# Two token tiles of the output projection written ahead of the last head of the first attention, and each tile's mixed heads loaded during the tile before it

## The chip, the cores and the metric

The kernel runs on one core of one Trainium2 chip. A core has five engines with instruction streams of their own: TensorE (matrix products, into PSUM), VectorE, ScalarE, GpSimd and SyncE; in the profile they are PE, DVE, ACT, POOL and SP, and PEld is TensorE's loading of the stationary operand. SyncE only issues DMAs here; GpSimd issues DMAs and does some elementwise work. Each engine runs its instructions in the order in which they stand in its stream, and waits at an instruction until the semaphores it needs are there. The metric is the device time of one execution in microseconds (us).

## The reference

A decoder block over 2048 tokens of width 1024, in float32, depth 1:

```python
ada = c_act @ ada_w[l] + ada_b[l]                  # shift, scale, gate of both sub-layers
h = rms_norm(x, pre_norm_mix[l]) * (1.0 + sc_a) + sh_a
proj = h @ w_in                                     # one projection for both groups of heads
go = gla_chunked(gq, gk, gv, g_log)                 # 4 heads, gated linear attention
go = from_heads(rms_norm(go, gla_norm)) * jax.nn.silu(g_og)
do = diff_attention(dq, dk, dv, lam)                # 4 heads, (softmax1 - lam * softmax2) @ V, causal
do = from_heads(rms_norm(do, diff_norm) * (1.0 - lambda_init))
y = jnp.concatenate([go, do], axis=-1) @ w_out      # the output projection
x = x + gt_a * rms_norm(y, post_norm_mix[l])
h = rms_norm(x, pre_norm_mlp[l]) * (1.0 + sc_m) + sh_m
y = jnp.square(jax.nn.relu(h @ w_up[l])) @ w_down[l]
x = x + gt_m * rms_norm(y, post_norm_mlp[l])
```

The output projection of a token needs all eight mixed heads of that token. An attention head of a block of 128 queries reads the keys and values of all tokens up to the block's end.

## The kernel before

Float32 products are made of three products of split operands (high × high, high × low, low × high), each of 128 × 128 by up to 512 columns. The 2048 tokens are 16 **token tiles** of 128 and four **groups** of 512 (group t has tiles 4t to 4t + 3).

The stages, in the order in which they are written: the input projection with the linear attention for groups 0 and 1, then for groups 2 and 3; the differential attention of groups 0 and 1 (the *first attention*, begun among the last input projections); the output projection, most of it written among the differential attention of groups 2 and 3 (the *second attention*); the rest of the output projection; the MLP (from L1035 on). The change concerns only the attentions and the output projection.

**An attention** (`attention`, L171) is a generator. Its steps are (group t, head h, block j of 128 queries), and a step of group t has t + 1 chunks of 512 keys. Each turn of the innermost loop is a *tick*, after which the generator yields: scores of one chunk of the present step on TensorE (`qk`, `S`, L214), whose PSUM bank VectorE moves out with the running maximum (L219, or L222 for the chunk on the diagonal); then, for the step two steps back (`lag` 2), the transposes of the probabilities of one chunk (`turn`, L263), copied out by ScalarE (L265), and one tick later the products with V (`pv`, `O`, L274). After the last chunk of a step come the exponentials on ScalarE (L232) and the combination of the two softmaxes on VectorE (L238). When the last block of a head is done, `norm` (L279) makes squares on ScalarE, a root and `don` on VectorE (L289); two ticks later `finish` (L292) transposes `don` (L297), splits it (L299, L300), stores it to the scratch tensor `mixS` through GpSimd's queue (L302), and enters the head (t, h) in the set `finished`. Keys, values and queries are loaded by SyncE two steps ahead (L190, L192, L202).

**The output projection** (`out_proj`, L915) is a generator with 16 steps for a token tile: two halves `b` of 512 columns, eight rows `k` of w_out, each step with three matmuls (`Y`, L931 to L933). Ahead of a tile's steps stand the load of its mixed heads (`mx`, L921; in two parts for tiles 12 to 15, the last head by itself) and of the residual `xt` (L923), both on SyncE's queue. `mx` has two buffers; `xt` and `yt` share three with the raw rows of w_out. The two halves of a tile take two PSUM banks of one tag, of which there are two, so that the next tile's first matmul needs this tile's eviction. Behind the matmuls: squares on ScalarE (L936), a root and two evictions `wyt` on VectorE (L944), the sum with the residual on GpSimd (L946; on VectorE from tile 11 on), the store of x1, a second norm (L950, L952) and the store of `xnS`.

**What sets the order.** The program text interleaves generators by hand. `interleave` (L1003) takes one tick of the attention and then as many projection steps as are due: two a tick for the first 48 ticks of the second attention, then 1.5, at most 11 tiles (`TB`), and none while the next tile in the order `TOKS` (L964) isn't `ready`, which means that all four heads of its group are in `finished`. By the time `interleave` begins on the first attention, all but its last three ticks have been written: two a step of the last input projection (L867), two a row of w_out as this is split (L905). `prep_first` (L966), also driven a tick at a time, makes the first operands of the MLP out of finished tiles; it waits for counts of projection steps.

The order on the engines isn't quite the written one. A scheduler in the program builder places the instructions: among those that it reckons ready, it takes the one written first, so that an instruction written later can stand earlier in an engine's stream. That order is fixed before the kernel runs.

Of the kernel before, what the change touches and what calls it, by code (L numbers as in the profile page):

```python
# [9 lines left out]
F32 = mybir.dt.float32  # L10
F32R = mybir.dt.float32r
# [8 lines left out]
P = 128  # L20
# [3 lines left out]
NH = 4  # L24
# [3 lines left out]
NTOK = S // P  # L28
# [6 lines left out]
AT0 = 2  # L35
GA1 = 4
WL = 2
RA = 2.0
RB = 2.0
RC = 1.5  # L40
GA0 = 22
# [8 lines left out]
def tile_hybrid_block(  # L50
# [3 lines left out]
    nc = tc.nc  # L54
# [12 lines left out]
    mixS = [dram.tile([P, 4, 2 * NH, 2, P], F32, name=f"mixS{t}") for t in range(NT)]  # L67
# [49 lines left out]
    def rsqrt_col(pool, ss, n, inv_n, tag):  # L117

        y = pool.tile([P, n], F32, tag=tag + "y", name=tag + "y", bufs=2)
        nc.scalar.activation(y, ss, AF.Ln, scale=inv_n, bias=eps_c)  # L120
        nc.scalar.activation(y, y, AF.Exp, scale=-0.5)
        v = pool.tile([P, n], F32, tag=tag + "v", name=tag + "v", bufs=2)
        nc.vector.tensor_scalar(v, ss, inv_n, EPS, op0=ALU.mult, op1=ALU.add)

        w = pool.tile([P, n], F32, tag=tag + "w", name=tag + "w", bufs=2)
        nc.vector.tensor_tensor(w, y, y, op=ALU.mult)
        nc.vector.scalar_tensor_tensor(w, w, -0.5, v, op0=ALU.mult, op1=ALU.mult)
        r = pool.tile([P, n], F32, tag=tag + "r", name=tag + "r", bufs=2)
        nc.vector.scalar_tensor_tensor(r, w, 1.5, y, op0=ALU.add, op1=ALU.mult)
        return r  # L130
# [37 lines left out]
    finished = set()  # L168
# [273 lines left out]
    def run(g, n=None):  # L442

        while n is None or n > 0:
            if next(g, run) is run:
                return False
            n = None if n is None else n - 1
        return True
# [416 lines left out]
    at = attention((0, 1), sa, 1024, 6, pp, atags, 3, 3, 2)  # L865
# [26 lines left out]
    sw = c1.enter_context(tc.tile_pool(name="p1w", bufs=2, side="left", reuse_waits="tile"))  # L892
# [11 lines left out]
    for k in range(NK):  # L904
# [7 lines left out]
        if k + 3 < NK:  # L912
            load_wo(k + 3)

    def out_proj(tiles):  # L915

        for tk in tiles:
            assert all((tk // 4, h) in finished for h in range(NH))
            mx = sw.tile([P, 2 * NH, 2, P], F32R, tag="mx", name="mx", bufs=2)
            for ks in (slice(0, 7), slice(7, 8)) if tk >= 12 else (slice(0, 8),):  # L920
                nc.sync.dma_start(mx[:, ks].bitcast(F32), mixS[tk // 4][:, tk % 4, ks])  # L921
            xt = sw.tile([P, D], F32, tag="wx", name="wxt", bufs=3)
            nc.sync.dma_start(xt, x[tk * P:(tk + 1) * P, :])  # L923
            yps = []
            ss = sw.tile([P, 2], F32, tag="wss", name="wss", bufs=2)
            for b in range(2):
                yp = pp.tile([P, 512], F32, tag=("C" if tk > 12 and tk % 2 else "A"), name="Y",
                             bufs=4 if tk > 12 and tk % 2 else 2)
                cs = slice(512 * b, 512 * b + 512)
                for k in range(NK):  # L930
                    nc.tensor.matmul(yp, mx[:, k, 0, :], wohi[k][:, cs], start=(k == 0), stop=False)  # L931
                    nc.tensor.matmul(yp, mx[:, k, 0, :], wolo[k][:, cs], start=False, stop=False)  # L932
                    nc.tensor.matmul(yp, mx[:, k, 1, :], wohi[k][:, cs], start=False, stop=(k == NK - 1))  # L933
                    yield
                junk = sw.tile([P, 512], BF16, tag="wjunk", name="wjunk", bufs=1)
                nc.scalar.activation(junk, yp, AF.Square, accum_out=ss[:, b:b + 1])  # L936
                yps.append(yp)
            s1 = sw.tile([P, 1], F32, tag="ws1", name="ws1", bufs=2)
            nc.vector.tensor_tensor(s1, ss[:, 0:1], ss[:, 1:2], op=ALU.add)
            r = rsqrt_col(sw, s1, 1, 1.0 / D, "wr")  # L940
            yt = sw.tile([P, D], F32, tag="wx", name="wyt", bufs=3)
            for b in range(2):
                cs = slice(512 * b, 512 * b + 512)
                nc.vector.scalar_tensor_tensor(yt[:, cs], yps[b], r, gtg[:, cs], op0=ALU.mult, op1=ALU.mult)  # L944
            eng = nc.vector if tk >= 11 else nc.gpsimd
            eng.tensor_tensor(xt, xt, yt, op=ALU.add)  # L946
            nc.gpsimd.dma_start(x1S[tk], xt)

            s2 = sw.tile([P, 1], F32, tag="ws2", name="ws2", bufs=2)
            nc.scalar.activation(yt, xt, AF.Square, accum_out=s2)  # L950
            r2 = rsqrt_col(sw, s2, 1, 1.0 / D, "wq")
            nc.vector.tensor_scalar(yt, xt, r2, None, op0=ALU.mult)  # L952
            nc.gpsimd.dma_start(xnS[tk // 8][:, tk % 8], yt.rearrange("p (k c) -> p k c", c=P))
# [7 lines left out]

    TOKS = (0, 4, 1, 5, 2, 6, 3, 7) + tuple(range(8, 16))  # L964

    def prep_first(pool, tag):  # L966


        for n in range(16):
            i, k = n // 4, n % 4  # L970
            while len(wsteps) < 32 * (i + 1) + 4:
                yield
            raw = pool.tile([P, 2, 2, P], F32, tag="prq", name="xnq", bufs=2)
            for j in range(2):
                nc.gpsimd.dma_start(raw[:, j], xnS[0][:, 4 * j + i].rearrange("p (e k) c -> p e k c", e=2)[:, :, k, :])
            for _ in range(3):
                yield
            ps = pp.tile([P, 2, 2, P], F32, tag=tag, name="ntr", bufs=4)
            for e in range(2):
                for j in range(2):  # L980
                    nc.tensor.transpose(ps[:, e, j, :], raw[:, j, e, :], ident)
            bt = pool.tile([P, 2, 2, P], F32, tag="prq", name="hBq", bufs=2)
            for e in range(2):
                kk = k + 4 * e
                nc.scalar.activation(bt[:, e], ps[:, e], AF.Identity, bias=cols[:, 24 + kk:25 + kk],
                                     scale=prem[:, 1, kk:kk + 1])
# [12 lines left out]

    TB = 11  # L1000
    op = out_proj(TOKS[:TB])

    def interleave(at, first, rate, later, pre=None):  # L1003


        due, i = 0.0, 0
        while run(at, 1):
            due += rate if i < first else later
            while due >= 1.0:
                if len(wsteps) == 16 * TB or not ready(TOKS[len(wsteps) // 16]):  # L1010
                    due = 0.0
                    break
                run(op, 1)
                wsteps.append(1)
                due -= 1.0
            if pre is not None:
                run(pre, 1)
            i += 1

    wsteps = []  # L1020

    def ready(tk):
        return all((tk // 4, h) in finished for h in range(NH))

    interleave(at, 0, RA, RA)
    cA.close()
    cA = ExitStack()
    sa = cA.enter_context(tc.tile_pool(name="pA1", bufs=2, side="right", reuse_waits="tile"))
    at = attention((2, 3), sa, S, 6, pp, atags, 5, 5, 2)
    pre = prep_first(sa, "C")  # L1030
    interleave(at, 48, RB, RC, pre)
    run(op)
    run(pre)
# [109 lines left out]


    op = out_proj(TOKS[TB:])
    fetch_op(0)
    run(op, 14)
# [74 lines left out]
    n = len(usteps)  # L1222
    ready_ops = {}
    prep_todo = [(k, hf) for k in range(4) for hf in range(2)]
    for s, (g, c, wi, p) in enumerate(usteps):
        i = WORD[wi]
# [17 lines left out]
        nm, first = BANK[i]  # L1244
# [320 lines left out]
```

## Time and profile before

| what | value |
|---|---|
| time, median of 3 runs | 2588.66 us (2583.26 to 2590.06) |
| time of the profiled execution | 2586.39 us |
| its span, first to last instruction | 2584.7 us |
| mean granted TensorE clock | 0.983 |
| first and last `Y` matmul | 833.7 us, 1318.4 us |
| issues of `mx` loads | 20, from 824.2 to 1304.4 us |

The profile is of one execution. A busy engine is one that has an instruction under way; the idle time in front of an instruction is put down to the instruction or DMA that came last of those it waited for. The granted clock is the share of TensorE's full clock that it had in a stretch. Times in the trace are counted from the span's start.

### The profile page before, as it was taken

The page shows a single profiled execution, that of the slowest core. Times are in us where ns is not written, and L with a number is a line of the kernel's source. Part 1 is how long each engine was busy: PE and PEld are TensorE (multiplying, and loading weights), DVE is VectorE, ACT ScalarE, POOL GpSimd, SP SyncE. Part 2 cuts the span into 40 slices and gives each one's busy share as a digit, 9 for nine tenths or more (in the row PEclk, how much of TensorE's full clock was granted, in tenths as well). Part 3 has the DMA queues.
Part 4 walks back from the last instruction along what each step waited for, and adds up shares of the span by engine and source line. Part 5 has one row for each costly group of instructions (what it writes and reads, how often), then busy time and mean ns, then how long its engine had stood idle before and what let it go on. Part 6 is the DMA issues. An engine that isn't in the chain of part 4 may idle for free.

```text
span 2584.7 us, 35418 instructions
## 1 busy us (share of the span) xinstructions
PE 2464.8 (95%) x12532; PEld 2050.6 (79%) x12532; DVE 1593.1 (62%) x3111; ACT 1150.2 (45%) x2185; POOL 442.9 (17%) x654
## 2 busy tenths in 40 slices
PE   5899999999998899999999999999999999999998
PEld 4777787877787688888778888788888888788886
DVE  6535855247864677777577767866664445543756
ACT  4352224313444565566555555645553333222444
POOL 2211322102321123332012322112111000100000
PEclk8999999999999999999999999999999999999999
DMA  7354551444844766665475655744438767855856
GB/s 263 110 186 134 192 188 58 131 133 149 253 135 154 221 200 204 214 208 170 170 249 199 229 197 175 234 145 167 142 136 285 264 201 239 277 172 166 288 167 209
DMA packets 218792, 491.61 MB, mean 190 GB/s; under 512 B 24848, under 2 KB 78800, under 8 KB 217072
## 3 DMA queue, kind: packets, MB, share of 16 engines
q1 hardware_dynamic: 170000, 329.12, 40.3%
q0 software_dynamic: 48608, 160.16, 16.7%
q8 instruction: 100, 1.64, 0.3%
q14 instruction: 84, 0.69, 0.1%
HBM read 329.79 MB, written 159.39 MB: 189 GB/s over the span
## 4 chain that ended last, share of the span: by engine, by line
PE 41%; issue 17%; DMA 3%; POOL 3%; DVE 2%; ACT 2%; POOLq 0%; SPq 0%; DVEq 0%; ACTq 0%
PE dn L1428 4%; PE dn L1430 4%; PE dn L1429 4%; PE upY L1253 2%; PE upY L1251 2%; PE upY L1252 2%; PE S L214 2%; PE O L274 2%; PE Y L933 2%; PE Y L931 2%; PE Y L932 2%; PE upX L1253 2%; PE upV L1251 2%; PE upV L1253 2%; PE upV L1252 2%
## 5 line engine op out<-in xcount | busy, mean ns | idle before, releaser
L1428 PE MATMUL dn<-dnhi,uhi 128*128 128x512 f32 x880 | 344.5, 391 | 3.9 <-DVE du L1408 3.9
L1430 PE MATMUL dn<-dnhi,ulo 128*128 128x512 f32 x880 | 344.1, 391 | 1.1 <-DVE ulo L1357 1.1
L1429 PE MATMUL dn<-dnlo,uhi 128*128 128x512 f32 x880 | 344.2, 391 | 0.0
L1355 ACT CAST uhi<-us 128x1024 fp32r<-128x1024 f32 (+1 forms) x126 | 118.7, 944 | 359.8 <-PE dn L1429 343.2
L1357 DVE TENSOR_TENSOR ulo<-us,uhi 128x1024 fp32r<-128x1024 f32 (+1 forms) x126 | 136.9, 1087 | 160.6 <-ACT uhi L1355 155.9
L537 PE MATMUL projt<-hThi,whi 128*128 128x512 f32 x512 | 207.2, 405 | 0.6 <-DVE cols L416 0.6
L538 PE MATMUL projt<-hTlo,whi 128*128 128x512 f32 x512 | 206.3, 403 | 0.0
L539 PE MATMUL projt<-hThi,wlo 128*128 128x512 f32 x512 | 202.0, 395 | 2.2 <-DVE wlo L471 2.2
L1428 PEld LDWEIGHTS dn<-dnhi,uhi 128*128 128x128 f32 x880 | 165.9, 189 | 39.8 <-issue 3.6
L1430 PEld LDWEIGHTS dn<-dnhi,ulo 128*128 128x128 f32 x880 | 166.0, 189 | 36.6 <-DVE ulo L1357 1.5
L1429 PEld LDWEIGHTS dn<-dnlo,uhi 128*128 128x128 f32 x880 | 166.0, 189 | 35.3
L232 ACT ACTIVATE P<-P,nm 128x128 f32<-128x128 f32 (+15 forms) x128 | 153.7, 1201 | 48.9 <-DVE nm L222 48.1
L214 PE MATMUL S<-K,q 128*128 128x512 f32 (+3 forms) x640 | 169.7, 384 | 2.6 <-issue 1.6
L1133 ACT CAST wuhi<-wA 128x512 fp32r<-128x512 f32 x160 | 99.1, 619 | 163.9 <-PE upV L1252 69.2
L274 PEld LDWEIGHTS O<-V,PTs 128*128 128x128 f32 x1088 | 141.5, 193 | 26.4 <-ACT PTs L265 15.6
L274 PE MATMUL O<-V,PTs 128*128 128x128 f32 x1088 | 151.9, 280 | 8.4 <-ACT PTs L265 4.9
L1253 PE MATMUL upY<-hhi,wulo 128*128 128x512 f32 x384 | 151.6, 395 | 2.0 <-DVE wulo L1134 2.0
L1251 PE MATMUL upY<-hhi,wuhi 128*128 128x512 f32 x384 | 151.7, 395 | 0.2 <-ACT wuhi L1133 0.2
L1252 PE MATMUL upY<-hlo,wuhi 128*128 128x512 f32 x384 | 151.5, 394 | 0.0
L551 PE MATMUL projn<-whi,hThi 128*128 128x256 f32 x512 | 147.7, 288 | 3.4 <-DVE cols L416 2.6
L552 PE MATMUL projn<-wlo,hThi 128*128 128x256 f32 x512 | 146.9, 287 | 0.0
L553 PE MATMUL projn<-whi,hTlo 128*128 128x256 f32 x512 | 145.5, 284 | 0.0
(334 smaller groups left out, 5727.1 us busy)
## 6 DMA issues: line engine op xcount, KB each, us to landing
us<-uS SPq DMA_DIRECT2D x94, 512.0 KB, 4.2
wA<-in_w_up_dram SPq DMA_DIRECT2D x128, 256.0 KB, 3.1
uS<-t POOLq DMA_DIRECT2D x128, 256.0 KB, 3.2
wraw<-in_w_in_dram SPq DMA_DIRECT2D x48, 512.0 KB, 4.6
uS<-c POOLq DMA_DIRECT2D x96, 256.0 KB, 3.1
K<-kS SPq DMA_DIRECT2D x40, 512.0 KB, 5.4
wds<-in_w_down_dram SPq DMA_DIRECT2D x78, 256.0 KB, 4.2
adaraw<-in_ada_w_dram SPq DMA_DIRECT2D x32, 512.0 KB, 4.0
```

The costliest lines, as they stand in the source:

```text
L214: nc.tensor.matmul(ps[:, :wd], qt[:, m, hl, qs], Kc[ci][:, m, :wd], start=(hl == 0), stop=(hl == 1))
L232: nc.scalar.activation(Ps[m][:, :width], Ps[m][:, :width], AF.Exp, scale=-1.0, bias=nms[m][:, t:t + 1], accum_out=sums[:, 0, m:m + 1])
L274: nc.tensor.matmul(outs[t, h][:, j, :], pt[:, kb % 4, :], Vc[g][:, kb % 4, :], start=(kb == 0), stop=(kb == nb - 1))
L537: nc.tensor.matmul(ps, whi[k][:, cs], hi[:, k, :], start=(k == 0), stop=False)
L538: nc.tensor.matmul(ps, whi[k][:, cs], lo[:, k, :], start=False, stop=False)
L539: nc.tensor.matmul(ps, wlo[k][:, cs], hi[:, k, :], start=False, stop=(k == NK - 1))
L1251: nc.tensor.matmul(ps, whi[:, k, :], hi[:, k, :], start=(first and k == 0), stop=False, skip_group_check=not first)
L1252: nc.tensor.matmul(ps, whi[:, k, :], lo[:, k, :], start=False, stop=False, skip_group_check=not first)
L1253: nc.tensor.matmul(ps, wlo[:, k, :], hi[:, k, :], start=False, stop=(k == 3), skip_group_check=not first)
L1428: nc.tensor.matmul(banks[t], uhi[:, tk], whi, start=first, stop=False, skip_group_check=on)
L1429: nc.tensor.matmul(banks[t], uhi[:, tk], wlo, start=False, stop=False, skip_group_check=on)
L1430: nc.tensor.matmul(banks[t], ulo[:, tk], whi, start=False, stop=last, skip_group_check=on)
```

## The change

The load of `mx` becomes a function of its own, `load_mx`. In a tile's step (b, k) = (1, 0), the ninth of 16, the text now asks for the next tile's `mx`, if the heads of its group are finished. The order of the tiles begins 0, 1, 4, 5 in place of 0, 4, 1, 5, and the counts in `prep_first` are those that fit it. In the last three ticks of the first attention, `interleave` is replaced by a loop that writes 16 projection steps after each tick until 32 are written: tile 0 after the first, tile 1 after the second, both ahead of the third, in which `finish` of head (1,3) falls. In the second attention, a tile whose `mx` hasn't been asked for is asked for in a tick, and its first step is written three ticks later at the earliest.

```diff
-RA = 2.0
...
+    def load_mx(tk):
+
+        if tk in mxs or not ready(tk):
+            return
+        mxs[tk] = sw.tile([P, 2 * NH, 2, P], F32R, tag="mx", name="mx", bufs=2)
+        for ks in (slice(0, 7), slice(7, 8)) if tk >= 12 else (slice(0, 8),):
+            nc.sync.dma_start(mxs[tk][:, ks].bitcast(F32), mixS[tk // 4][:, tk % 4, ks])
+
     def out_proj(tiles):
 
-        for tk in tiles:
-            assert all((tk // 4, h) in finished for h in range(NH))
-            mx = sw.tile([P, 2 * NH, 2, P], F32R, tag="mx", name="mx", bufs=2)
-            for ks in (slice(0, 7), slice(7, 8)) if tk >= 12 else (slice(0, 8),):
-                nc.sync.dma_start(mx[:, ks].bitcast(F32), mixS[tk // 4][:, tk % 4, ks])
+        for n_, tk in enumerate(tiles):
+            load_mx(tk)
+            mx = mxs.pop(tk)
...
+                    if (b, k) == (1, 0):
+                        at_ = TOKS.index(tk) + 1
+                        if at_ < NTOK:
+                            load_mx(TOKS[at_])
                     yield
...
-    TOKS = (0, 4, 1, 5, 2, 6, 3, 7) + tuple(range(8, 16))
+    TOKS = (0, 1, 4, 5, 2, 6, 3, 7) + tuple(range(8, 16))
...
-            while len(wsteps) < 32 * (i + 1) + 4:
+            while len(wsteps) < (48, 64, 96, 128)[i] + 4:
...
+    def op_step():
+
+        if len(wsteps) == 16 * TB or (len(wsteps) % 16 == 0 and TOKS[len(wsteps) // 16] not in mxs):
+            return False
+        run(op, 1)
+        wsteps.append(1)
+        return True
+
+    def interleave(at, first, rate, later, pre):
+
+
+        due, i, asked = 0.0, 0, {}
         while run(at, 1):
             due += rate if i < first else later
+            n = len(wsteps) // 16
+            if len(wsteps) % 16 == 0 and n < TB and TOKS[n] not in mxs:
+                load_mx(TOKS[n])
+                asked[n] = i
             while due >= 1.0:
-                if len(wsteps) == 16 * TB or not ready(TOKS[len(wsteps) // 16]):
+                n = len(wsteps) // 16
+                if (len(wsteps) % 16 == 0 and i < asked.get(n, -3) + 3) or not op_step():
                     due = 0.0
                     break
...
-    interleave(at, 0, RA, RA)
+    load_mx(0)
+    while run(at, 1):
+        for _ in range(16):
+            if len(wsteps) < 32:
+                op_step()
```

More of the change, by code (lines that the diff above doesn't have):

```diff
@@ L913, in tile_hybrid_block, with ready @@
             load_wo(k + 3)
-    def out_proj(tiles):
-        for tk in tiles:
-            assert all((tk // 4, h) in finished for h in range(NH))
-            mx = sw.tile([P, 2 * NH, 2, P], F32R, tag="mx", name="mx", bufs=2)
-            for ks in (slice(0, 7), slice(7, 8)) if tk >= 12 else (slice(0, 8),):
-                nc.sync.dma_start(mx[:, ks].bitcast(F32), mixS[tk // 4][:, tk % 4, ks])
+    mxs = {}
+    def ready(tk):
+        return all((tk // 4, h) in finished for h in range(NH))
+    def load_mx(tk):
[4 more added lines that the diff above has]
+            nc.sync.dma_start(mxs[tk][:, ks].bitcast(F32), mixS[tk // 4][:, tk % 4, ks])
+    def out_proj(tiles):
+        for n_, tk in enumerate(tiles):
+            load_mx(tk)
+            mx = mxs.pop(tk)
             xt = sw.tile([P, D], F32, tag="wx", name="wxt", bufs=3)
@@ L1001, in tile_hybrid_block @@
     op = out_proj(TOKS[:TB])
-    def interleave(at, first, rate, later, pre=None):
-        due, i = 0.0, 0
+    wsteps = []
+    def op_step():
[6 more added lines that the diff above has]
+        due, i, asked = 0.0, 0, {}
         while run(at, 1):
             due += rate if i < first else later
+            n = len(wsteps) // 16
+            if len(wsteps) % 16 == 0 and n < TB and TOKS[n] not in mxs:
+                load_mx(TOKS[n])
+                asked[n] = i
             while due >= 1.0:
-                if len(wsteps) == 16 * TB or not ready(TOKS[len(wsteps) // 16]):
+                n = len(wsteps) // 16
+                if (len(wsteps) % 16 == 0 and i < asked.get(n, -3) + 3) or not op_step():
                     due = 0.0
                     break
-                run(op, 1)
-                wsteps.append(1)
                 due -= 1.0
-            if pre is not None:
-                run(pre, 1)
+            run(pre, 1)
             i += 1
-    wsteps = []
-    def ready(tk):
-        return all((tk // 4, h) in finished for h in range(NH))
-    interleave(at, 0, RA, RA)
+    load_mx(0)
[3 more added lines that the diff above has]
+                op_step()
     cA.close()
```

## The prediction, on record before the result

> **What bounds the kernel now.** I read the page first, then the waits of TensorE around the end of the first attention, then the instructions in order of time there, and last the busy time by stretches.
>
> ```profile
> span 2584.7 us, 35418 instructions
> ## 1 busy us (share of the span) xinstructions
> PE 2464.8 (95%) x12532; PEld 2050.6 (79%) x12532; DVE 1593.1 (62%) x3111; ACT 1150.2 (45%) x2185; POOL 442.9 (17%) x654
> ```
>
> The first view of waits is of 780 to 1000 us, the second of 1000 to 1330 us (total, times, longest):
>
> ```profile
> engine line waited for: us in total, times, longest us
> PE dps L297 <- DVE don L289: 7.1, 2, 6.5
> PE O L274 <- PEq L873: 3.1, 1, 3.1
> PE Y L931 <- DMA mx<-mixS: 2.7, 1, 2.7
> ```
>
> ```profile
> PE Y L931 <- DVE wyt L944: 5.5, 3, 2.8
> PE dps L297 <- DVE don L289: 3.1, 3, 1.9
> PE Y L931 <- DMA mx<-mixS: 2.4, 1, 2.4
> ```
>
> TensorE is busy for 95% of the span, so only its idle time can be won: 2584.7 − 2464.8 = 119.9 us over the whole kernel. The change touches the stretch from the last two heads of the first attention to the last tiles of the output projection. There the waits name what can move: 6.5 us, the longest wait for `don`, and 2.7 us for a tile's mixed heads at the seam between the attentions; 5.5, 3.1 and 2.4 us further on.
>
> ```profile
> 872.67 2.05 PE L274 MATMUL O<-V,PTs 128*128 128x128 f32 x16 [0.24 <-ACT PTs L265]
> 881.20 1.08 PE L297 MATMUL dps<-ident,don 128*128 128x128 f32 x4 [6.47 <-DVE don L289]
> 881.93 7.11 PE L214 MATMUL S<-K,q 128*128 128x512 f32 x24
> 889.22 0.49 PE L214 MATMUL S<-K,q 128*128 128x512 f32 x1 [0.17 <-DVE P L219]
> 892.42 0.50 PE L931 MATMUL Y<-wohi,mx 128*128 128x512 f32 x1 [2.71 <-DMA mx<-mixS]
> ```
>
> ```profile
> 872.04 0.16 DVE L129 SCALAR_TENSOR_TENSOR wrr<-wrw,wry 128x1 f32<-128x1 f32 x1
> 872.24 1.41 DVE L944 SCALAR_TENSOR_TENSOR wyt<-Y,wrr,gtg 128x512 f32<-128x512 f32 x2
> ...
> 878.91 0.75 DVE L952 TENSOR_SCALAR wyt<-wxt,wqr 128x1024 f32<-128x1024 f32 x1
> ```
>
> ```profile
> 884.09 0.73 POOL L302 DMA_DIRECT2D mixS<-dmo  x1 [3.59 <-DVE dmo L300]
> ...
> 887.45 0.34 SPq L921 DMA_DIRECT2D mx<-mixS  x1
> ```
>
> These are instructions in order of time (start, us, engine, line; idle time before in brackets) on TensorE, on VectorE, and the two DMA issues of GpSimd and SyncE. The last PV products (L274) of head (1,3) end at 872.67 + 2.05 = 874.72. TensorE then has nothing until that head's norm (`don`, L289) releases its transposes (L297) at 881.20: 6.47 us idle. It then runs 24 score matmuls of the second attention. The head is stored at 884.09, the load of tile 4's mixed heads is issued at 887.45, and tile 4's first matmul starts at 892.42 after 2.71 us idle. Before the change tile 4 is the second in order, and it can't come before head (1,3) is stored. So at 874.72 no projection work is left that could fill the stall.
>
> ```profile
> core 0: us, PE busy (x) PEld busy (x) DVE busy (x) ACT busy (x) POOL busy (x), PEclk, DMA share, GB/s
> 875.00:881.00 6.00, 0.00 (x0) 0.00 (x0) 2.66 (x11) 3.24 (x14) 2.21 (x3) 0.91 0.65 181
> 881.00:893.00 12.00, 8.91 (x32) 7.19 (x33) 9.00 (x30) 5.94 (x9) 2.24 (x4) 0.76 0.64 227
> 893.00:905.00 12.00, 12.00 (x61) 10.23 (x60) 5.82 (x16) 3.46 (x8) 0.00 (x0) 0.86 0.78 223
> 905.00:1065.00 160.00, 156.87 (x950) 136.20 (x949) 118.26 (x346) 95.71 (x203) 46.84 (x57) 1.00 0.65 205
> 1065.00:1082.00 17.00, 12.89 (x79) 10.61 (x78) 14.17 (x40) 10.94 (x28) 5.13 (x6) 1.00 0.53 165
> ...
> 1215.00:1262.00 47.00, 46.29 (x319) 40.49 (x318) 30.94 (x86) 30.65 (x57) 4.23 (x4) 1.00 0.22 71
> ```
>
> The granted clock, by stretches, falls to 0.91 in the stall and 0.76 and 0.86 behind it, and is 1.00 from 905 on.
>
> **The change, part by part.**
>
> *Two tiles ahead of the last head.* The first attention has 16 ticks (yields) for token group 0, 2 × 16 for group 1, four for the lag and three to drain: 55. 18 × 2 and 8 × 2 of them are written before the projection begins, so three are left. Today they carry two projection steps each, 6 of tile 0; the rest of tile 0 is written behind them, yet its eviction (`wyt`, L944) at 872.24 shows that all its 48 matmuls had run by then: the scheduler draws forward what is ready. The changed text writes tile 0 and then tile 1 there, ahead of `finish` of (1,3). Tile 1 needs only group 0, so 48 matmuls become free for the stall.
>
> ```profile
> 904.73 1.08 PE L214 MATMUL S<-K,q 128*128 128x512 f32 x4
> 905.66 0.38 PE L274 MATMUL O<-V,PTs 128*128 128x128 f32 x2
> ```
>
> ```profile
> 1076.34 0.39 PE L933 MATMUL Y<-wohi,mx 128*128 128x512 f32 x1
> 1076.57 0.40 PE L931 MATMUL Y<-wohi,mx 128*128 128x512 f32 x1
> ```
>
> Tile 1's price is 48 × 0.23 us (1076.57 − 1076.34) = 11.0 us of TensorE. Its banks are those of tile 0, two of one tag, free when tile 0's `wyt` pair ends at 872.24 + 1.41 = 873.65; just in time for 874.72. Its load needs the second `mx` buffer, which nobody holds then. So the 6.47 us are filled, and since tile 1 is written ahead of `finish`, I expect all of it to go first: the transposes of (1,3) move from 881.20 to 874.7 + 11.0 = 885.7, 4.5 us late. TensorE has done 11.0 us of work that it otherwise does later at full load (905 to 1065: 156.87 busy of 160). Term: 4.5 − 11.0 = **−6.5 us**.
>
> *The ramp behind it.* What is late next is the store of (1,3), 4.5 us, and so tile 4's load and first matmul: 892.4 + 4.5 = 896.9. SyncE's queue waits for that store as before; behind the load stand K, V and q of later steps. Best: tile 1 is spread so that neither the 2.71 us nor the slow clock returns. The 24 score matmuls took 7.11 us; at the pace of 905.66 − 904.73 = 0.93 us for four they take 5.6, so the best is −2.7 − 1.5 = −4.2 us. Worst: TensorE, at full clock, runs out of scores earlier and waits longer for tile 4 (25 scores × 0.2325 = 5.8 us from 885.7 + 0.7 = 886.4, to 892.2; 896.9 − 892.2 = 4.7 against 2.7, so +2.0), and tile 1's tail on VectorE stands ahead of the score evictions: 1.41 + 0.75 + nine small operations at 0.16 (the row of 872.04 is one) = 3.6 us. Sum +5.6 us. VectorE was busy 9.00 of 12 us here, so 3.0 of the 3.6 fit its gaps, which speaks against the worst; that VectorE also paces the scores speaks against the best. I take the middle, **+0.7 us**.
>
> The Trainium skill, "TensorE: Matmul & The Clock Gate" (sections "Why this matters for your kernels" and "What's actually happening"), says to allow no gaps of more than about 3 us between matmuls, or the clock falls to half; an estimate by its half-rate window of about 3.4 us is 1.7 us lost per such gap. The trace agrees: 1.5 us lost behind 6.47 us. By that rule alone the filled stall would give 8.2 us instead of 6.5.
>
> *The gap this opens.* The second attention has 123 ticks. Before, steps run from 6 at two a tick for 48 ticks, then 1.5: tile 8 (which needs group 2) begins in tick 65, the eleventh tile ends in tick 97, with no stop. After, they start at 32, three ticks late; eight tiles (128 steps) are used up in tick 51. Head (2,3) is finished in tick 57, tile 8 may begin three ticks after: ticks 52 to 59 carry no projection. The eleventh tile ends in tick 91, six earlier.
>
> ```profile
> 1219.05 1.18 PE L214 MATMUL S<-K,q 128*128 128x512 f32 x4
> ...
> 1221.31 1.18 PE L214 MATMUL S<-K,q 128*128 128x512 f32 x4
> ```
>
> ```profile
> 1072.81 0.50 PE L931 MATMUL Y<-wohi,mx 128*128 128x512 f32 x1 [2.18 <-DVE wyt L944]
> ...
> 1079.60 0.66 PE L297 MATMUL dps<-ident,don 128*128 128x128 f32 x4 [1.93 <-DVE don L289]
> ```
>
> An unfilled tick lasts 1221.31 − 1219.05 = 2.26 us, and in 1215 to 1262, where few are filled, TensorE is still busy 46.29 of 47 and VectorE 30.94. A filled tick is longer only by its matmuls, so projection taken out of one place costs nothing by itself: the work that hides it is the attention's own on TensorE. What cover is gone: around head (2,3) the trace shows 2.18 us (a tile's banks not yet evicted) and 1.93 us (`don`); between them, from 1072.81 to 1079.60 − 1.93 = 1077.67, 4.9 us of work, projection for the most part. Best: both waits go, −4.1; worst: those 4.9 us turn into wait, +4.9. I take **0**, since the scheduler can put scores there. The shorter fill at the end likewise 0: tiles 11 and 12 are free to be drawn forward.
>
> *Loads one tile ahead.* Same 20 loads and bytes, same queue, issued in the middle of the tile in front. TensorE waited for `mx` only twice, 2.7 and 2.4 us, and both times the load itself waited for a head's store (884.09, then 887.45; the other is tile 12's last head). An earlier issue can't help: **0**. Steps for `prep_first` start two or three ticks earlier by the new thresholds (52 steps in tick 12, before 36 in tick 14): 0.
>
> Sum: −6.5 + 0.7 = −5.8. The profiled execution took 2586.39 us (span 2584.7), the median of the runs shown is 2588.66. 2586.39 − 5.8: forecast **2580.6 us**, 0.31% under that median.
>
> **The rivals.**
>
> *The full clock and the second wait too* (2575.7): the ramp comes out at its best, −6.5 − 4.2 = −10.7. For it: the rows of 0.76 and 0.86. Against it: the scores are also paced by VectorE, busy 9.00 of 12. It is what the skill's rule on gaps leans to.
>
> *The stall only moves* (2585.5): the ramp comes out at its worst, −6.5 + 5.6 = −0.9. For it: tile 4 can't start before (1,3) is stored, and that is later.
>
> *The softmax side sets the pace where filler is missing* (2600.0): slower. If ticks don't shrink when the filler leaves, the eight empty ticks and six at the end cost their missing length. A filled one has 1.5 steps, 1.5 × 3 × 0.23 = 1.04 us: 14 × 1.04 = 14.5; the norm of (2,3) loses its 4.9 us of cover; −5.8 + 14.5 + 4.9 = +13.6. It decides when VectorE's work per tick passes 2.26 us. For it: VectorE was busy 14.17 of 17 us in 1065 to 1082, just where the gap falls. Against it: 30.94 of 47 later, with the same widths.
>
> *The change doesn't do what it says*: tile 1's matmuls stay behind the transposes in TensorE's order; then 2586.4. It would take tile 0's eviction coming later than today's 873.65. I count it with the rival that moves the stall.
>
> **How the numbers follow.** 0.3% of 2588.66 is 7.8 us, about what a measurement of this kernel can tell from no change: faster is below 2580.9, slower above 2596.4. Chances: forecast 0.46, full clock 0.18, moved or none 0.19, softmax pace 0.17. The forecast lies at the edge; on its own it runs from 2576 to 2585, half of it below the edge: 0.23 faster, 0.23 same. Faster 0.23 + 0.18 = 0.41; same 0.23 + 0.19 = 0.42; slower 0.17. Range: the best of all terms is −6.5 − 4.2 − 4.1 = −14.8, 2571.6, so 2571; upward I go to 2593, about the sum with the worst ramp and the worst gap (−6.5 + 5.6 + 4.9 = +4.0, 2590.4) and something over, part of the way to the slow rival, which leaves some 0.14 above and 0.05 below.
>
> **What would show it.** Tile 1's `Y` matmuls stand between 873 and 886 us and the wait of L297 for `don` (6.5 us) is gone: the first step. The granted clock is 1.00 through 875 to 890: the rival of the full clock. Tile 4's first matmul still waits for `mx`, at some 897: the ramp. Between ticks 52 and 59 no `Y` on TensorE, and ticks of 2.3 us there: the gap is free; ticks of 3 us or a long wait for `don` or L219: the slow rival. I am wrong if the seam keeps an idle stretch above 5 us, or if the idle time of TensorE from 905 on grows by more than the 6 us won.

## The result, and the profile after

The changed kernel takes 2601.81 us in the median (2594.05 to 2608.49), the kernel before beside it 2587.34 us (2581.20 to 2592.73): a ratio of 1.0056, with a 95% interval of 1.0037 to 1.0074. It is slower by 14.5 us, where 2580.6 us were forecast; the range ended at 2593. The profiled execution took 2597.73 us, 11.3 us more than the one before.

The page of the changed kernel, its head:

```profile
span 2596.0 us, 35440 instructions
## 1 busy us (share of the span) xinstructions
PE 2466.1 (95%) x12532; PEld 2050.8 (79%) x12532; DVE 1590.1 (61%) x3111; ACT 1150.3 (44%) x2185; POOL 443.4 (17%) x654
```

TensorE is busy as long as before (2466.1 us against 2464.8), so what was added is idle time: 2596.0 − 2466.1 = 129.9 us, against 119.9. Lines have moved: `Y` is L941 to L943 now, `wyt` L958, GpSimd's add L960, the second-norm square on ScalarE L964, `dps` L296, `S` L213, `mx` L925, the residual load L933; in an experiment they may lie some lines further, and the names tell.

TensorE at the seam of the changed kernel, in order of time:

```profile
869.86 2.05 PE L273 MATMUL O<-V,PTs 128*128 128x128 f32 x16 [0.24 <-ACT PTs L264]
871.67 0.48 PE L941 MATMUL Y<-wohi,mx 128*128 128x512 f32 x1
...
882.66 0.60 PE L296 MATMUL dps<-ident,don 128*128 128x128 f32 x4
894.72 7.05 PE L213 MATMUL S<-K,q 128*128 128x512 f32 x24 [11.46 <-DMA q<-qS]
...
902.63 0.50 PE L941 MATMUL Y<-wohi,mx 128*128 128x512 f32 x1 [0.19 <-DMA mx<-mixS]
```

The wait for `don` is gone. Tile 1's 48 matmuls begin at 871.67, and the transposes of head (1,3) stand right behind the last of them, at 882.66, with no wait. But the second attention's scores, which followed within a microsecond before, now wait 11.46 us for q. In this view of SyncE's queue (first of the changed kernel, then of the kernel before) a row's length holds the time that the issue waited:

```profile
852.47 28.07 SPq L933 DMA_DIRECT2D wxt<-in_x_dram  x3
880.59 0.54 SPq L189 DMA_DIRECT2D K<-kS  x1
...
884.43 9.57 SPq L201 DMA_DIRECT2D q<-qS  x8
```

```profile
855.33 6.30 SPq L923 DMA_DIRECT2D wxt<-in_x_dram  x2
861.68 0.54 SPq L190 DMA_DIRECT2D K<-kS  x1
...
865.84 9.29 SPq L202 DMA_DIRECT2D q<-qS  x8
```

The waits of that queue from 840 to 900 us, in the changed kernel (total, times, longest):

```profile
SPq L933 <- DMA xnS<-wyt: 21.3, 1, 21.3
```

Before, two residual loads stood ahead of the second attention's K, V and q; now it is three, because tile 1 has moved ahead of the seam and tile 4's residual was drawn forward behind it. The buffer that the third one fills is that of tile 0's `wyt`, and this is free only when tile 0's normed row (`xnS`) has been stored. In the text of both kernels tile 4's load stands behind the second attention's first K, V and q; the scheduler placed it ahead of them. The issue waited 21.3 us, and everything behind it on the queue waited too: the first K went out at 880.59 instead of 861.68, the q loads at 884.43 instead of 865.84.

Busy time by stretches in the changed kernel, with the columns of before (after the busy times of the five engines: granted clock, DMA share, GB/s), and then the stretch from 1074 to 1109 in the kernel before:

```profile
875.00:881.00 6.00, 6.00 (x28) 4.99 (x27) 2.56 (x10) 2.03 (x10) 0.53 (x1) 1.00 0.41 160
881.00:893.00 12.00, 2.26 (x13) 1.66 (x11) 4.35 (x13) 3.30 (x9) 5.29 (x7) 0.70 0.98 309
893.00:905.00 12.00, 9.91 (x35) 7.81 (x36) 8.15 (x28) 4.52 (x7) 0.44 (x1) 0.74 1.06 350
905.00:1065.00 160.00, 154.82 (x915) 133.18 (x914) 112.46 (x334) 93.72 (x200) 44.91 (x54) 0.99 0.64 203
1074.00:1109.00 35.00, 28.02 (x165) 23.25 (x164) 28.57 (x83) 21.54 (x45) 11.47 (x16) 0.90 0.60 195
1092.00:1098.00 6.00, 5.82 (x26) 5.44 (x27) 3.52 (x10) 2.94 (x7) 4.44 (x4) 0.56 0.29 98
1154.00:1160.00 6.00, 5.81 (x26) 5.62 (x27) 2.71 (x8) 3.45 (x5) 0.73 (x1) 0.60 0.47 175
```

```profile
1074.00:1109.00 35.00, 32.79 (x209) 28.73 (x208) 27.47 (x74) 19.59 (x35) 10.65 (x14) 1.00 0.66 222
```

875 to 881, empty before, is full at a clock of 1.00, and the next 12 us are empty instead (2.26 busy, clock 0.70). The Trainium skill, "TensorE: Matmul & The Clock Gate" ("Why this matters for your kernels"), has the clock fall after an idle stretch of more than about 3 us; this trace agrees: 0.70 and 0.74 behind and around 11.46 us of idle time. From 1074 to 1109 TensorE is idle for 35.00 − 28.02 = 7.0 us, at a clock of 0.90, where before it was 35.00 − 32.79 = 2.2 us, at 1.00. The clock fell there too, to 0.56 from 1092 to 1098, behind two waits of 2.36 and 2.77 us with some 1.2 us of work between them (next view); neither is as long as the about 3 us of the Trainium skill's rule, so gaps shorter than that weren't safe here.

The waits of TensorE in the second attention and after it (1000 to 1340 us) of the changed kernel, and in order of time its waits in that stretch that matter:

```profile
PE dps L296 <- DVE don L288: 8.0, 3, 4.7
PE O L273 <- ACT PTs L264: 4.4, 7, 2.4
```

```profile
1088.26 1.16 PE L273 MATMUL O<-V,PTs 128*128 128x128 f32 x8 [2.36 <-ACT PTs L264]
...
1092.18 1.11 PE L296 MATMUL dps<-ident,don 128*128 128x128 f32 x4 [2.77 <-DVE don L288]
...
1093.80 2.05 PE L213 MATMUL S<-K,q 128*128 128x512 f32 x4
...
1108.46 0.50 PE L941 MATMUL Y<-wohi,mx 128*128 128x512 f32 x1 [0.85 <-DMA mx<-mixS]
...
1154.19 1.09 PE L296 MATMUL dps<-ident,don 128*128 128x128 f32 x4 [4.71 <-DVE don L288]
...
1330.99 0.40 PE L943 MATMUL Y<-wohi,mx 128*128 128x512 f32 x1
```

No `Y` runs in some 34 us ahead of 1108.46: the gap, where 2.36 us for the PTs and 2.77 us for head (2,3)'s `don` lie open. The wait of 4.71 us at 1154.19 lies outside it. It comes from a tile's tail, on ScalarE:

```profile
1149.27 1.06 ACT L964 ACTIVATE wyt<-wxt 128x1024 f32<-128x1024 f32 x1 [4.88 <-POOL wxt L960]
...
1150.32 0.35 ACT L284 ACTIVATE djunk<-O,rsd 128x128 bf16<-128x128 f32 x1
```

ScalarE's stream holds tile 8's second-norm square (L964) ahead of the last of four squares of a head's norm (L284). The square waits 4.88 us for GpSimd's residual add, the head's norm waits behind it though its own data are there, and TensorE waits for the `don`.

The two traces split at three points, the last PV products of head (1,3) (872.67 before, 869.86 after), the first score of the second attention (881.93, 894.72) and the last `Y` (1318.43, 1330.99). From the first to the second: 9.3 us before, 24.9 after, of which 11.0 are tile 1's work: +4.6. From the second to the third: 436.5 and 436.3 us, though those 11.0 us of work are no longer in it: +10.8. The stage in front took 2.8 us less and the one behind 1.3 less; why isn't shown. Sum: 4.6 + 10.8 − 2.8 − 1.3 = 11.3, the difference of the spans.

### The profile page after: what moved, and what is told of

Read it like the earlier page. It is cut to its first block, busy times and chain, and to the rows that moved or that the text cites. A ratio compares the mean times of both kernels' runs of the same rounds, so it can differ in the third digit from the quotient of the medians.

```text
span 2596.0 us, 35440 instructions
## 1 busy us (share of the span) xinstructions
PE 2466.1 (95%) x12532; PEld 2050.8 (79%) x12532; DVE 1590.1 (61%) x3111; ACT 1150.3 (44%) x2185; POOL 443.4 (17%) x654
## 4 chain that ended last, share of the span: by engine, by line
issue 30%; PE 25%; POOL 6%; DMA 3%; DVE 2%; ACT 1%; SPq 0%; POOLq 0%; DVEq 0%; ACTq 0%
PE dn L1457 4%; PE dn L1455 4%; PE dn L1456 4%; PE S L213 2%; PE O L273 2%; POOL uS L1206 2%; POOL uS L1237 2%; PE PT L262 1%; PE Y L941 1%; PE Y L943 1%; PE Y L942 1%; POOL wdS L1335 1%; DMA mx<-mixS 1%; POOL uS L1245 1%; PE upY L1278 1%
## 5 line engine op out<-in xcount | busy, mean ns | idle before, releaser
L213 PE MATMUL S<-K,q 128*128 128x512 f32 (+3 forms) x640 | 173.1, 389 | 12.8 <-DMA q<-qS 11.5
```

Of the source, the lines that this page charges most:

```text
L213: nc.tensor.matmul(ps[:, :wd], qt[:, m, hl, qs], Kc[ci][:, m, :wd], start=(hl == 0), stop=(hl == 1))
```

## The experiments

Three theories, then. **Queue:** the third residual load ahead of K, V and q costs 11.5 us. **Gap:** ticks without projection cost, since nothing covers the attention's own waits. **Tail:** a tile's tail, which passes from engine to engine, holds the attention on an engine that executes in order. The rivals are those recorded with each run. All runs leave the computation whole. Ratios are against runs of the kernel before on the same chip; its median beside them lay between 2586.25 and 2588.97 us, so that a difference of two medians and that of their ratios can be some 3 us apart. Differences below are of medians, where nothing else is said.

| run | median, us | ratio to before, 95% interval |
|---|---|---|
| the change | 2601.8 | 1.0056 [1.0037, 1.0074] |
| e_qfirst: queue edit | 2597.9 | 1.0048 [1.0032, 1.0064] |
| e_rate: gap closed, 1.6 steps a tick | 2587.8 | 1.0006 [0.9994, 1.0018] |
| e_both: queue edit and 1.6 | 2582.3 | 0.9982 [0.9970, 0.9994] |
| e_tail: and tile 1's tail later | 2575.9 | 0.9966 [0.9949, 0.9982] |
| e_tail_vec: and all adds on VectorE | 2572.1 | 0.9942 [0.9924, 0.9960] |
| e_align: the change, tile 8's add on VectorE | 2593.8 | 1.0025 [1.0014, 1.0036] |
| e_gap2: gap closed in another way | 2592.4 | 1.0022 [1.0005, 1.0038] |
| e_tail2: that, queue edit, tile 1's tail later | 2585.8 | 0.9993 [0.9979, 1.0008] |
| d2_order: new order, no loads ahead | 2609.2 | 1.0090 [1.0070, 1.0111] |
| d1_loads: loads ahead, old order | 2587.0 | 1.0002 [0.9993, 1.0012] |
| c_rate: kernel before, 1.6 | 2612.2 | 1.0103 [1.0087, 1.0118] |
| c_rate_vec: that, all adds on VectorE | 2597.0 | 1.0031 [1.0019, 1.0043] |

**The queue alone (e_qfirst).** `issue_after` keeps an instruction behind another one of its engine.

```diff
-                        nc.sync.dma_start(qt[64 * d:64 * d + 64, :, hl, :].bitcast(F32), rows)
+                        lastq[0] = nc.sync.dma_start(qt[64 * d:64 * d + 64, :, hl, :].bitcast(F32), rows)
...
-            nc.sync.dma_start(xt, x[tk * P:(tk + 1) * P, :])
+            with tc.issue_after(lastq[0].ins) if tk == TOKS[2] else ExitStack():
+                nc.sync.dma_start(xt, x[tk * P:(tk + 1) * P, :])
```

> The changed kernel with one DMA moved in SyncE's queue: the residual load of the third tile in order (tile 4's wxt) is issued behind the first K, V and q of the second attention instead of ahead of them. Nothing else is changed. Queue theory: in the changed kernel that load waits 21.3 us for the buffer of tile 0's wyt, and K, V and q wait behind it; TensorE then idles 11.46 us for q ahead of the second attention. Then the wait goes, up to 3 us come back as a wait for tile 4's mixed heads (they were stored at the same time as before), and the time falls from 2601.8 by 8.5 to 11.5 us to 2590 to 2593. Rival (the time is lost in the second attention where projection is missing, and the seam is only where it is first seen): the wait goes but the time stays above 2598.

The wait for q went, as the queue theory has it, but the time fell by only 3.9 us, and the two intervals overlap. The trace shows why, on TensorE, VectorE and GpSimd of this run:

```profile
880.95 2.05 PE L274 MATMUL O<-V,PTs 128*128 128x128 f32 x16 [0.24 <-ACT PTs L265]
...
894.11 1.63 PE L214 MATMUL S<-K,q 128*128 128x512 f32 x6
896.12 0.73 PE L214 MATMUL S<-K,q 128*128 128x512 f32 x2 [0.38 <-DVE dmo L300]
904.34 2.08 PE L214 MATMUL S<-K,q 128*128 128x128 f32 x5 [7.49 <-DVE P L219]
```

```profile
896.56 1.41 DVE L960 SCALAR_TENSOR_TENSOR wyt<-Y,wrr,gtg 128x512 f32<-128x512 f32 x2
901.61 0.15 DVE L122 TENSOR_SCALAR wqv<-ws 128x1 f32<-128x1 f32 x1 [3.63 <-ACT wyt L966]
...
902.92 0.75 DVE L968 TENSOR_SCALAR wyt<-wxt,wqr 128x1024 f32<-128x1024 f32 x1
903.59 0.68 DVE L219 TENSOR_SCALAR_CACHE_REDUCE P<-S 128x512 f32<-128x512 f32 x1
```

```profile
898.06 2.33 POOL L962 TENSOR_TENSOR wxt<-wxt,wyt 128x1024 f32<-128x1024 f32 x1 [0.97 <-DVE wyt L960]
```

K, V and q are there, eight score matmuls run, and then TensorE waits 7.49 us for the first eviction (`P` from `S`). VectorE has it behind tile 1's whole tail: the `wyt` pair, and then four small operations and `wyt` from `wxt` (902.92), which need ScalarE's square of what GpSimd adds from 898.06 on. VectorE stands idle for 3.63 us in the middle of that. So two waits lay side by side at the seam, 11.46 us long and 7.49 us long, and taking the longer one away left the shorter: 11.46 − 7.49 = 4.0, about what was won. (From the last PV products to tile 4's first matmul, at 909.95 here, it is 29.0 us against 32.8 in the changed kernel: 3.8 us less.) Neither theory had this; it is the tail theory's first case.

**The gap alone (e_rate), and both (e_both).**

```diff
-RB = 2.0
+RB = 1.6
```

> The changed kernel with the first rate of projection in the second attention lowered from 2 steps a tick to 1.6, so that the tiles of groups 0 and 1 last until group 2's last head is nearly done and no eight ticks stay without projection. The order on SyncE's queue at the seam stays as in the changed kernel. Gap theory (the empty ticks with their waits for PTs and don cost): 5 to 9 us less, 2593 to 2597. Rival (empty ticks shrink to the attention's own work, as the prediction had it): no gain, 2600 to 2603, the same waits elsewhere. Queue theory: the 11.5 us wait for q stays in both.

> The changed kernel with both edits: the third tile's residual load behind the first K, V and q of the second attention, and 1.6 steps of projection a tick. If queue and gap each cost what the two theories say and add up: 2601.8 less 8.5 to 11.5 less 5 to 9, 2581 to 2588, at or under the kernel before. If only the queue costs: as the run with the queue edit alone, 2590 to 2593. If only the gap costs: as the run with the rate alone.

Closing the gap won 14.0 us, more than the 5 to 9 expected, with the wait for q still there. Two views of that run, waits of TensorE from 880 to 1000 us and the busy time of the stretch in which the change has its gap:

```profile
PE S L213 <- DMA q<-qS: 11.2, 1, 11.2
```

```profile
1074.00:1109.00 35.00, 34.97 (x212) 29.81 (x211) 26.64 (x76) 23.50 (x47) 11.07 (x14) 1.00 0.78 258
```

From 1074 to 1109 TensorE is now busy for 34.97 of 35 us, against 28.02. The wait of 4.71 us behind tile 8's tail is gone too: tile 8 ends elsewhere. With both edits the gains add up, 14.0 and then 5.5 us more, to a ratio under 1; 2582.3 lies in the range expected.

**The tail at the seam (e_tail).**

```diff
+                with tc.issue_after(evs[1].ins) if tk == TOKS[1] else ExitStack():
+                    nc.vector.scalar_tensor_tensor(yt[:, cs], yps[b], r, gtg[:, cs], op0=ALU.mult, op1=ALU.mult)
...
+            with tc.issue_after(evs[-1].ins) if tk == TOKS[1] else ExitStack():
+                r2 = rsqrt_col(sw, s2, 1, 1.0 / D, "wq")
+                nc.vector.tensor_scalar(yt, xt, r2, None, op0=ALU.mult)
```

`evs` holds the score evictions of groups 2 and 3 as they are written.

> The run with the queue edit and the rate of 1.6, and on VectorE tile 1's tail put behind the first score evictions of the second attention: its wyt pair behind the second eviction, its second norm (wqv, wqw, wqr, wyt from wxt) behind those written by then. Nothing else is changed. Theory of the tail: once K, V and q are there, TensorE waits 7.5 us at the seam for the score eviction L219, because VectorE executes in order and holds tile 1's second norm, which waits for GpSimd's add and ScalarE's square, ahead of the first eviction. Then this wait goes; up to 4 us of it may come back as a wait for tile 4's mixed heads, which are stored no earlier: 2582.3 less 3.5 to 7.5, 2575 to 2579. Rival (the scores at the seam are held by something else, or the mixed heads set tile 4's start in any case and everything behind it): 2581 to 2583.

TensorE and VectorE at the seam of this run:

```profile
891.90 0.44 PE L215 MATMUL S<-K,q 128*128 128x128 f32 x2 [0.56 <-DVE P L220]
...
893.18 2.94 PE L215 MATMUL S<-K,q 128*128 128x512 f32 x12 [0.23 <-DVE P L220]
899.24 0.76 PE L946 MATMUL Y<-wohi,mx 128*128 128x512 f32 x1 [3.11 <-DMA mx<-mixS]
```

```profile
891.15 0.69 DVE L220 TENSOR_SCALAR_CACHE_REDUCE P<-S 128x512 f32<-128x512 f32 x1
...
895.48 1.40 DVE L964 SCALAR_TENSOR_TENSOR wyt<-Y,wrr,gtg 128x512 f32<-128x512 f32 x2
...
901.31 0.14 DVE L122 TENSOR_SCALAR wqv<-ws 128x1 f32<-128x1 f32 x1
```

The first eviction runs at 891.15, the `wyt` pair behind eight evictions at 895.48, the second norm at 901.31 without a wait on VectorE. The 7.5 us have shrunk to 0.56 us; 3.11 us come back as the wait for tile 4's mixed heads. The median fell by 6.4 us to 2575.9, within what was expected; its interval overlaps that of e_both a little, and from the last PV products of (1,3) to the last `Y` its trace is 4.8 us shorter than that of e_both.

**The tail in mid-attention (e_align).**

```diff
-            eng = nc.vector if tk >= 11 else nc.gpsimd
+            eng = nc.vector if tk >= 11 or tk == 8 else nc.gpsimd
```

> The changed kernel with one instruction moved: tile 8's residual add runs on VectorE instead of GpSimd. Queue at the seam and gap stay. Alignment theory: in the changed kernel ScalarE holds tile 8's second-norm square, which waits 4.9 us for GpSimd's add, ahead of a head's last square, and TensorE waits 4.7 us for that head's don with a slower clock behind it; with the add early that wait goes: 2601.8 less 4 to 6, 2596 to 2598. Rival (the wait only moves to the next tile or to VectorE, or hides other work): 2600 to 2603.

ScalarE of this run, where the changed kernel waited 4.88 us:

```profile
1145.48 0.37 ACT L284 ACTIVATE djunk<-O,rsd 128x128 bf16<-128x128 f32 x1
...
1146.41 1.04 ACT L964 ACTIVATE wyt<-wxt 128x1024 f32<-128x1024 f32 x1
```

One add on another engine won 8.0 us of the 14.5. The head's fourth square now comes first, and TensorE's wait of 4.71 us is gone. That is more than the wait. Part of the rest is the clock behind it: 0.60 from 1154 to 1160 in the changed kernel, 1.00 in this run from 1152 to 1158. An estimate from the row of that stretch is 5.81 × 0.40 = 2.3 us, which with the 4.71 makes 7.0; some 1 us stays open. Since e_rate also removed this wait, its 14.0 us aren't the gap's price alone: 14.0 − 8.0 = 6.0 us are left for the gap, if the two add (4.9 by the ratios). That they add wasn't tested.

**The control for the rate (c_rate), and the control with its adds on VectorE (c_rate_vec).** The kernel before with `RB = 1.6`; then with `eng = nc.vector` for all tiles as well.

> The kernel before with the rate of 1.6 steps a tick alone, as a control for the rate. Gap theory: the kernel before has no ticks without projection, so the lower rate gains nothing: 2584 to 2592, and the 14 us that it gained in the changed kernel are the price of the gap that the change opened. Rival (1.6 suits the attention better in any kernel, gap or not): 2572 to 2578.

> The kernel before with the rate of 1.6 (2612.2 us, 25 slower than before) and every tile's residual add on VectorE instead of GpSimd. The rate's trace shows ScalarE waiting 5.9 and 5.5 us for that add, with exponentials and PTs copies behind, and TensorE waiting 4.1 and 3.2 us for the PTs. Theory of the tail: what the lower rate costs in the old order are mostly such meetings of a tile's tail with the attention on ScalarE's queue in order; the add on VectorE shortens them, and 7 to 15 us come back, 2597 to 2605. Rival (thin filler: the softmax side sets the pace and TensorE waits whatever the tails do): 2608 to 2616.

Neither theory had a loss of 25 us in the control. So 1.6 steps a tick isn't good in itself, which was to be tested, but what it costs there was a surprise. Its trace shows the tail again, ScalarE first and TensorE beneath:

```profile
1011.11 1.06 ACT L950 ACTIVATE wyt<-wxt 128x1024 f32<-128x1024 f32 x1 [5.93 <-POOL wxt L946]
```

```profile
1014.20 2.08 PE L274 MATMUL O<-V,PTs 128*128 128x128 f32 x8 [4.12 <-ACT PTs L265]
```

ScalarE waits 5.93 us for GpSimd's add, with an exponential and the PTs behind it. With the adds on VectorE the ratio falls from 1.0103 to 1.0031: 0.72%, some 19 us of 27 (15 of 25 by the medians), came back, and TensorE's waits for the PTs from 880 to 1340 us fell from 11.0 to 2.1 us. So most of the loss hung on the adds on GpSimd; how much of it were such meetings, and how much a shorter tail would win at any rate, isn't separated. The same edit on the fastest kernel:

> The fastest run so far (queue edit, rate 1.6, tile 1's tail behind the score evictions: 2575.9 us) with every tile's residual add on VectorE. In its trace no wait of TensorE behind such an add is left beyond 1.9 us. Theory of the tail: little is left to win, and VectorE has 1.2 us more work a tile: 2573 to 2578. Rival (VectorE, which also evicts the scores, is the engine that paces): 2579 or more.

It won 3.8 us more in the median, a little more than expected, with overlapping intervals, and is the fastest kernel of the study, 0.58% under the kernel before. What the adds alone would do to the kernel before at its own rate wasn't tried.

**The gap closed in another way (e_gap2), with the seam mended (e_tail2).**

```diff
-    interleave(at, 48, RB, RC, pre)
+    interleave(at, 24, RB, RC, pre)
```

> The changed kernel with the gap closed in another way: 2 steps a tick for the first 24 ticks of the second attention instead of 48, then 1.5 as before. Steps 0 to 128 then end at about tick 60, where group 2's last head is done, as with 1.6 throughout, but at other places in between. The order on SyncE's queue at the seam stays. Gap theory: what the rate of 1.6 won, it won because no ticks stayed empty, so this wins the same, 2585 to 2592; up to 8 us more if a tile's second-norm square again meets a head's norm on ScalarE. Rival (1.6 steps a tick is itself what suits, by where tiles end and heads' norms fall): little is won, 2597 to 2603.

> The changed kernel with the queue edit, tile 1's tail behind the first score evictions, and 2 steps a tick for 24 ticks, then 1.5, in place of 1.6. If the three costs are separate, this stands under the run that closes the gap in this way alone by what queue and tail won at the rate of 1.6, 11.9 us: 2573 to 2580, as the run with 1.6. Rival (the seam's gains hang on what the second attention does after): 2582 or more.

The first won 9.4 us, a little less than the least that the gap theory expected. Its trace, too, has no wait as long as 4.71 us in the second attention, so that by the subtraction above only 9.4 − 8.0 = 1.4 us would be left for the gap. The second missed: queue and tail won 6.6 us here, not 11.9, and 2585.8 lies where its rival had it. The runs of e_gap2 lie from 2583.8 to 2599.9 us, more apart than those of any other edited kernel (those of the kernel before, beside it, from 2580.6 to 2598.3), so the difference of the two is poorly known; whether the seam's gain depends on what follows stays open.

**The two parts by themselves (d2_order, d1_loads).** The first is the changed kernel without the `load_mx` in step (1, 0) and without the three ticks of waiting; the second the kernel before with that `load_mx`.

> One part of the change alone: tiles 0 and 1 ahead of the first attention's last head in the new order, but each tile's mixed heads loaded when the tile begins, as before, and no three ticks of waiting for them. The third residual load stands ahead of K, V and q in SyncE's queue here too. Queue theory: the 11.5 us wait for q is there, 2599 to 2606, the loads one tile ahead being worth 0 to 4 us. Rival (the loads one tile ahead are what disturbs the queue): 2582 to 2590 and no long wait for q.

> The other part of the change alone: each tile's mixed heads loaded in the middle of the tile in front, with the old order of tiles and the old interleaving. Prediction on record: the two waits for mx of the kernel before are waits for a head's store, so an earlier issue gains nothing: 2584 to 2590. Rival (loads ahead are worth the 7 us that the new order loses without them, in the old order too): 2578 to 2582. A third: a load that waits for a store early in SyncE's queue holds the K, V and q behind it: above 2592.

In the old order the loads ahead change nothing that can be measured. In the new order the kernel without them is slower still (1.0090 against 1.0056, the intervals overlapping a little; 2609.2 us, 3 us above what was expected), and it waits for q too, on TensorE:

```profile
900.71 7.07 PE L213 MATMUL S<-K,q 128*128 128x512 f32 x24 [11.59 <-DMA q<-qS]
```

So the loss comes with the order of the tiles, not with the loads ahead.

## Why the prediction was wrong, step by step

**The stall is filled: right.** Tile 1's matmuls stand from 871.67 to 882.66 us, 11.0 us as reckoned, and the 6.47 us for `don` are gone. The term of −6.5 was there to be had: in e_qfirst, where q is there in time, the first score comes 894.11 − 880.95 = 13.2 us after the start of the last PV products, against 9.3 before, with 11.0 us more work between: 7.1 us won up to there.

**The ramp: the step that failed first.** The prediction followed one load on SyncE's queue, that of tile 4's `mx`: "SyncE's queue waits for that store as before; behind the load stand K, V and q of later steps." The load that mattered was the residual of the third tile in order, whose place in the queue the new order changed and whose buffer depends on tile 0's tail. It was counted neither as an issue nor as a wait, so +0.7 came out as +11.1 (the seam's +4.6 less the −6.5). The ends given, −4.2 to +5.6, were too narrow for a second reason: tile 1's tail on VectorE was costed by its busy time, 3.6 us. In e_qfirst it holds VectorE from 896.56 to 903.67, 7.1 us, because VectorE also stands still in it for GpSimd and ScalarE, and TensorE waits 7.49 us. Tile 4's first matmul came at 902.63, not at some 897. Both signs that the prediction had set for being wrong came: an idle stretch of 11.46 us at the seam (above 5), and from 905 us to the end 43.9 us of idle time on TensorE against 35.9 before (more than 6 added).

**The gap: the second.** "Projection taken out of one place costs nothing by itself" is half right. Where no wait is open, an unfilled tick is as short as reckoned; score groups of the changed kernel near the end:

```profile
1216.64 1.18 PE L213 MATMUL S<-K,q 128*128 128x512 f32 x4
1218.97 1.26 PE L213 MATMUL S<-K,q 128*128 128x512 f32 x4
1221.09 1.18 PE L213 MATMUL S<-K,q 128*128 128x512 f32 x4
```

2.33 and 2.12 us, against 2.26. But around head (2,3) projection was what covered 2.36 us for PTs and 2.77 us for `don`, near the worst end of +4.9 that the prediction had worked out and not taken. From 1074.23 to 1106.90 twelve score groups start 2.97 us apart on average, near the "ticks of 3 us" that the prediction had set as the sign of the slow rival; 6.1 us of it are the waits, and without them it is 2.4 us. "The scheduler can put scores there" failed: in TensorE's stream the next scores (1093.80) stand behind both waits. What the gap costs isn't settled: TensorE's idle time there grew by 4.8 us (7.0 against 2.2), and the runs leave 6.0 us for it by e_rate and 1.4 by e_gap2, if gap and tail add.

**Not in the sum at all: where the tails fall.** Moving the projection moved every later tile's end against the heads' norms. One such meeting, at 1154, cost 8.0 us by e_align. The prediction set VectorE's free time against tile 1's tail and had no term for ScalarE, which was busy for 44% of the span and still held TensorE up. The rate moves these meetings too: c_rate lost 25 us, so the gap and the tails can't be told apart by the rate alone.

**Loads one tile ahead at 0: right** for the old order (1.0002); in the new order they gave something back.

**The rivals.** The time lies 1.8 us from the slow rival's 2600.0, but not by its mechanism: 14.5 of its us were for ticks that don't shrink, and where nothing waits they do; only its 4.9 us for the lost cover of (2,3)'s norm came, as waits of 2.36 and 2.77. That the time comes so near is chance. Nearest in kind was "the stall only moves": it moved from `don` to q, at a place which that rival didn't name. With the queue, the gap and the tail at the seam mended the kernel takes 2575.9 us, in figure the 2575.7 of the rival of the full clock. That is chance too: the lower rate and the later tail are edits that this rival didn't have, and what the filled stall alone is worth in whole runs wasn't measured.

## What to carry to other kernels

When work is written earlier, list every DMA that is drawn forward with it and ask of each which buffer it waits for and what stands behind it in the same queue: one load that waits holds back those behind it, whoever needs them, as 21.3 us of waiting did here. Cost a chain that passes over several engines by its length from first to last, not by the busy time on one of them, and look at whatever it stands in front of. When a wait is taken away, look for the next shorter one that ran beside it before counting the gain.

## What the runs showed of the hardware

The same add of 128 × 1024 float32 values took 2.33 us on GpSimd (898.06, above) and 1.22 us on VectorE, in the run with all adds there:

```profile
928.79 1.22 DVE L966 TENSOR_TENSOR wxt<-wxt,wyt 128x1024 f32<-128x1024 f32 x1
```
